# Storing the low parts of shared weights in DRAM for the second half, and two steps of the convolution and the SSD decay on ScalarE

## The chip, the cores and the metric

One core of a Trainium2 chip runs the kernel alone. The metric is the device time of one execution in microseconds. A core has five engines with queues of their own: TensorE (PE, with its weight loads PEld), VectorE (DVE), ScalarE (ACT), GpSimd (POOL) and SyncE (SP), which here issues nearly all transfers. Each engine takes its instructions in order and waits on semaphores for the others.

## The reference

One decoder layer over 1024 tokens of width 2048, all in float32. One input projection feeds three causal token mixers; their outputs are joined, projected back and normalised with the residual.

```python
h = einsum('bld,dn->bln', x, w_in)
y_s5  = s5_mixer(...) * silu(s5_z)
qk    = silu(causal_dwconv(ml_qk, ml_conv_w, ml_conv_b))       # 4 taps
y_ml  = mlstm_mixer(q, k, ml_v, ...) * silu(ml_z)
xbc   = silu(causal_dwconv(ssd_xbc, ssd_conv_w, ssd_conv_b))   # 4 taps
y_ssd = rms_norm(ssd_mixer(xs, bs, cs, ssd_dt, ...) * silu(ssd_z), ssd_norm_g)
out   = einsum('bln,nd->bld', concatenate([y_s5, y_ml, y_ssd]), w_out)
x     = layer_norm(ALPHA * x + out, ln_g, ln_b)

# in ssd_mixer, per chunk of 128 tokens and per head:
seg  = a_cum[:, :, :, None] - a_cum[:, :, None, :]
lmat = exp(where(causal, seg, -inf))
```

## The kernel before, in words

The matrix products keep float32 accuracy by splitting: each operand becomes a high part, rounded to the type fp32r that TensorE takes, and a low part, the rest. A product is three matmuls: high by high, high by low, low by high. The helper `split` (lines 170 to 172) makes the parts: ScalarE casts the raw tile to the high part, VectorE subtracts that from the raw tile.

The program has four stages. The first, to about 680 us of the profiled execution, computes part of the projections with sums and differences of blocks; it is not touched. Then `half(0)` and `half(1)` each treat 512 tokens: six column tiles qk, then fourteen tiles xbc, each a projection followed by the four-tap convolution and SiLU, while the mLSTM and SSD mixers run in between as background pieces. Last, `outproj(0)` and `outproj(1)` multiply 512 tokens each with the output weights, in four blocks of 512 columns (nb 0 to 3), and normalise.

Weights come in units of 512 KB (128 rows by 1024 floats), in the order of the list `W.plan`. `Weights.next` hands one out and emits the next: a transfer from DRAM into a raw tile `w<n>r` (three buffers, shared with the raw activation tiles x1r, y0r and y1r), then the split into `w<n>h` and `w<n>l` (three buffers each). Units w123 to w162 serve half 0 and w163 to w202 serve half 1 with the same 40 pieces of weights. Units w203 to w234 serve output projection 0; w235 to w274 serve output projection 1, with the same 32 pieces, of which the last eight come twice: in the last column block, token tiles 0 and 1 are done first (`op13a`, w259 to w266), then tiles 2 and 3 (`op13b`, w267 to w274). Three units, w270 to w272, have buffers of their own (`W.spare`).

In `conv` (line 353) ScalarE copies the projection out of PSUM into `stg`, VectorE multiplies by the first tap and adds the bias (line 359), then adds three more taps (line 361); ScalarE applies SiLU.

In `ssd_super`, for each of six heads of a group, a row of cumulated decays is spread over all partitions (tile `A`). `sel` takes its exponential into `E`. `mask` subtracts the column's own cumulated decay in four pieces of 128x128, bounded above by 0 (VectorE, line 469, with the negated sums `NC` from `cumulate`), takes the exponential (ScalarE, line 470) and multiplies by the masked products `cbs`.

The order on each engine is set by a scheduler that simulates the program; the code gives the order of emission. In names such as s00A the digits are the half and the SSD group.

Of the kernel before, what the change touches and what calls it, by code (L numbers as in the profile page):

```python
# [13 lines left out]
ALU = mybir.AluOpType  # L14
# [25 lines left out]
def hybrid_trunk(ctx: ExitStack, tc: tile.TileContext, a: dict, out: bass.AP, dbg=None):  # L40
# [186 lines left out]
    class Weights:  # L227
# [5 lines left out]
        def emit(self):  # L233
            if self.at in self.spare:
                (src, shape), n = self.plan[self.at], f"w{self.at}"
                self.at += 1
                r = raw(src, shape, n + "r")
                th, tl = ([gt(f"{n}{x}{i}", dtype=F32R) for i in range(2)] for x in "hl")
                for i in range(2):
                    split(r[:, i], th[i], tl[i])  # L240
                self.ready.append((th, tl))
                return


            (src, shape, *more), n = self.plan[self.at], f"w{self.at}"
            before, after, key = more or ((), (), 0)
            if src is not None:
# [34 lines left out]
    W = Weights()  # L282

    def plan_c(t):
        W.plan += [(a["w_c"][t, u], (P, 8, P)) for u in range(2)]

    def plan_t(src, N):
        W.plan += [(src[u], (P, 2, N)) for u in range(8)]

# [63 lines left out]
    def conv(ps, halo, cw, cb, t, dest, nm):  # L353
# [4 lines left out]
        c = gt(nm + "cv")  # L358
        dve.tensor_scalar(out=c, in0=stg[:, 0:HT], scalar1=cw[:, t, 0:1], scalar2=cb[:, t:t + 1], op0=ALU.mult, op1=ALU.add)
        for j in range(1, 4):  # L360
# [32 lines left out]
    def cumulate(h, LC):  # L393
# [4 lines left out]
        NC = sp.tile([P, 4, 36], F32, name=n + "NC", tag="NC")  # L398
        dve.tensor_scalar_mul(NC.rearrange("p c k -> p (c k)"), ps[:, :144], -1.0)
        pr = pm(n + "r")  # L400
        for c in range(4):
# [12 lines left out]
        act.copy(out=ir, in_=pt[64:68, :])  # L414
        return NC, b, lf, ir


    def ssd_super(h, sgp, tiles, gx, ys):

        n = f"s{h}{sgp}"  # L420
        DT, NC = gx
        xs, BT, CT = tiles[0:3], tiles[3:5], tiles[5:7]
# [39 lines left out]
        def mask(k):  # L462
# [3 lines left out]
            for c in range(4):  # L466
                sl = slice(c * P, (c + 1) * P)

                dve.tensor_scalar(out=Lm[:, sl], in0=Lm[:, sl], scalar1=NC[:, c, hd:hd + 1], scalar2=0.0, op0=ALU.add, op1=ALU.min)
            act.activation(out=Lm, in_=Lm, func=AF.Exp)  # L470
            if k % 3 == 0:
# [993 lines left out]
    for h in range(2):  # L1465
# [4 lines left out]
        for t in sg_tiles(1)[:3]:  # L1470
            plan_c(t)
        plan_t(a["w_x4"], HT)
    for nb in (0, 1, 2, 3, 0, 1, 2, 3, 3):
        plan_t(a["w_out"][nb], HT)

# [3 lines left out]
    def half(h, X, Xn):  # L1479
# [4 lines left out]
        def pre():  # L1484
# [3 lines left out]
            yield  # L1488
            NC, b, lf, ir = cumulate(h, LC)
            gx.extend([DT, NC])  # L1490
            yield
# [227 lines left out]
```

## Time and profile before

| | |
|---|---|
| Median of 3 runs | 1612.53 us (1611.51 to 1612.76) |
| Profiled execution | 1610.04 us, span 1608.3 us |
| TensorE clock granted | 0.994 |
| Busy: TensorE, VectorE, ScalarE, GpSimd | 1579.1, 1120.7, 658.2, 80.3 us |
| DRAM traffic | 271.74 MB read, 57.28 MB written |

The span goes from the first to the last instruction that the profiler shows. A row of the profile names the line, the engine, the operation, and the tiles as out<-in. A group of instructions has its count, busy time and mean duration in ns, and after the bar the idle time of its engine just before it with what ended it; `PE ms L571 <- DVE sm L566: 1.2, 1, 1.2` in a list of waits says that TensorE's instruction writing ms at line 571 waited for VectorE's writing of sm, 1.2 us in total, once, 1.2 at longest. In a timeline the first number is the start in us, the second the duration. A transfer's row gives its size and the time from issue to landing.

### The profile page before, as it was taken

Reading aid. Unit: us, or ns where it says so; the run is one execution under the profiler, and the core shown is the slowest. Engines: PE = TensorE matmul, PEld = TensorE weight load, DVE = VectorE, ACT = ScalarE, POOL = GpSimd, SP = SyncE. Lnnn points to the kernel's source line nnn. Section 1 sums busy time; section 2 is a strip of 40 time slices with the busy share of each in tenths; the row PEclk is TensorE's granted clock in tenths of the full one; section 3 lists DMA queues with packets and bytes.
Section 4 is the critical chain, followed back from the end, with each engine's and each line's share of the span. In section 5 each row is a group of like instructions: output and inputs, shape, how many; then the busy total and the mean of one; then the engine's idle time right before and its main releaser. Section 6 shows DMA issues by size and latency. Waiting matters only on the chain. (4 is left out here: it accounts for less than half of the span.)

```text
span 1608.3 us, 21146 instructions
## 1 busy us (share of the span) xinstructions
PE 1579.1 (98%) x7688; PEld 1329.4 (83%) x7688; DVE 1120.7 (70%) x1844; ACT 658.2 (41%) x927; POOL 80.3 (5%) x183
## 2 busy tenths in 40 slices
PE   9999999999999999999999999999999999999996
PEld 7898988987988888778888888788887888888884
DVE  5678978878868786565646788685697753484348
ACT  4333242147345556543542546364354331321222
POOL 0000000000001110001100000010000000000000
PEclk9999999999999999999999999999999999999998
DMA  8988777987987768364434553452654453575345
GB/s 318 328 320 316 255 269 251 306 293 223 336 302 248 247 227 275 130 223 127 137 105 159 183 169 119 151 171 66 217 195 145 132 194 118 183 242 160 129 144 183
DMA packets 139304, 333.56 MB, mean 207 GB/s; under 512 B 24489, under 2 KB 41001, under 8 KB 139201
## 3 DMA queue, kind: packets, MB, share of 16 engines
q1 hardware_dynamic: 129792, 317.54, 59.1%
q10 hardware_dynamic: 9408, 14.68, 2.6%
q8 instruction: 60, 0.98, 0.2%
q14 instruction: 44, 0.35, 0.1%
HBM read 271.74 MB, written 57.28 MB: 205 GB/s over the span
## 5 line engine op out<-in xcount | busy, mean ns | idle before, releaser
L1297 DVE TENSOR_TENSOR e<-e,b 128x512 f32<-128x512 f32 (+1 forms) x72 | 43.9, 645 | 3.7 <-PE b L1372 3.2
L1556 DVE SCALAR_TENSOR_TENSOR r<-r,mv,ln_g 128x512 f32<-128x512 f32 x32 | 23.1, 742 | 0.0
L1557 DVE SCALAR_TENSOR_TENSOR r<-r,lrs,ln_b 128x512 f32<-128x512 f32 x32 | 23.0, 742 | 0.0
L1576 DVE BATCH_NORM_STATS2 bst<-r 128x6 f32<-128x512 f32 x32 | 20.8, 682 | 0.0
L362 ACT ACT_TABLE_LOAD x15 | 19.2, 1283 | 3.7 <-DVE qc00cv L361 3.4
L1052 POOL COPY s5m0up<-s5m0u 128x256 f32<-128x256 f32 x2 | 0.8, 398 | 316.2 <-DMA s5m0u<-s5u 316.2
L1297 DVE TENSOR_TENSOR f<-f,b1c 128x512 f32<-128x512 f32 x15 | 9.4, 682 | 8.7 <-ACT f L1350 8.7
L172 DVE TENSOR_TENSOR y1l<-y1r,y1h 128x1024 fp32r<-128x1024 f32 x8 | 9.8, 1222 | 7.5 <-ACT y1h L171 7.5
L1277 ACT ACTIVATE f<-f 128x512 f32<-128x512 f32 x20 | 12.1, 628 | 6.2 <-DVE f L1297 3.2
L171 ACT CAST y1h<-y1r 128x1024 fp32r<-128x1024 f32 x8 | 8.4, 1053 | 9.1 <-PE op03p L344 9.1
L779 DVE TENSOR_TENSOR s5small<-s5small 128x32 f32<-128x32 f32 (+2 forms) x66 | 11.2, 195 | 0.7
L1548 ACT ACTIVATE lrs<-lrs 128x1 f32<-128x1 f32 x8 | 1.6, 202 | 24.4 <-DVE lrs L1547 24.4
L1297 DVE TENSOR_TENSOR f<-f,b2c 128x512 f32<-128x512 f32 x5 | 3.4, 687 | 11.6 <-PE b2c L1444 11.6
L172 DVE TENSOR_TENSOR y0l<-y0r,y0h 128x1024 fp32r<-128x1024 f32 x8 | 9.8, 1221 | 2.3 <-ACT y0h L171 2.2
L172 DVE TENSOR_TENSOR x1l<-x1r,x1h 128x1024 fp32r<-128x1024 f32 x8 | 9.8, 1219 | 2.3 <-ACT x1h L171 2.3
L731 DVE TENSOR_TENSOR sgo<-sgo,mzs 128x384 f32<-128x384 f32 x16 | 8.9, 555 | 2.3 <-DMA mzs<-zg 2.1
L171 ACT CAST y0h<-y0r 128x1024 fp32r<-128x1024 f32 x8 | 8.4, 1046 | 4.9 <-PE xbc_13p L1531 4.8
L1271 ACT ACT_TABLE_LOAD x8 | 10.3, 1283 | 0.1
L1270 ACT ACT_TABLE_LOAD x7 | 9.0, 1283 | 2.4 <-ACT e L1271 2.4
L1305 ACT COPY e<-b 128x512 f32<-128x512 f32 (+1 forms) x12 | 6.7, 558 | 7.5 <-PE b L1372 7.5
L1160 DVE TENSOR_TENSOR gsg<-gsg,gsz 128x512 f32<-128x512 f32 x8 | 5.5, 683 | 6.0 <-DMA gsz<-s5z 6.0
L741 PEld LDWEIGHTS mf<-ident,sgo 128*128 128x128 f32 x48 | 5.7, 140 | 4.7 <-DVE sgo L731 3.8
(4696 smaller groups left out, 5741.1 us busy)
## 6 DMA issues: line engine op xcount, KB each, us to landing
xn<-in_x_dram SPq DMA_DIRECT2D x32, 256.0 KB, 5.5
out_dram<-r SPq DMA_DIRECT2D x32, 256.0 KB, 3.8
x1r<-in_xT_dram SPq DMA_DIRECT2D x8, 512.0 KB, 4.3
y0r<-mixT SPq DMA_DIRECT2D x8, 512.0 KB, 3.3
y1r<-mixT SPq DMA_DIRECT2D x8, 512.0 KB, 3.5
vd<-e SPq DMA_DIRECT2D x16, 192.0 KB, 4.0
szd<-f ACTq DMA_DIRECT2D x12, 256.0 KB, 3.0
vx<-vd SPq DMA_DIRECT2D x8, 384.0 KB, 4.3
```

The costliest lines, as they stand in the source:

```text
L171: act.copy(out=th, in_=raw)
L172: dve.tensor_sub(out=tl, in0=raw, in1=th.bitcast(F32))
L362: act.activation(out=dest, in_=c, func=AF.Silu)
L731: dve.tensor_mul(out=sg, in0=sg, in1=sz)
L779: eng.tensor_tensor(out=o, in0=i, in1=j, op=op)
L1270: act.activation(out=c[:, 0:256], in_=c[:, 0:256], func=AF.Silu)
L1271: act.activation(out=c[:, 256:512], in_=c[:, 256:512], func=AF.Sigmoid)
L1277: act.activation(out=c, in_=c, func=AF.Silu)
L1297: dve.tensor_tensor(out=o, in0=x, in1=y, op=op)
L1556: dve.scalar_tensor_tensor(out=o, in0=o, scalar=mv[:, 0:1], in1=lng[nb], op0=ALU.subtract, op1=ALU.mult)
L1557: dve.scalar_tensor_tensor(out=o, in0=o, scalar=rs, in1=lnb[nb], op0=ALU.mult, op1=ALU.add)
L1576: dve.bn_stats(out=st[t][:, nb, :], in_=r[t][nb])
```

## The change

Of the 80 units whose weights an earlier unit already had (w163 to w202, w235 to w274), the low part is no longer computed. The first unit with these weights stores its low part in DRAM (72 units, 512 KB each); a later one loads it into `w<n>l` while the raw tile is loaded and cast as before. The first convolution tap with its bias becomes an ACTIVATE with the function Identity on ScalarE. The decay bound becomes a Relu on ScalarE, with the sign turned: Relu(sum - A) and then Exp with scale -1; `cumulate` also keeps the sums unnegated, as PC.

```diff
--- before.py
+++ after.py
@@ -232,17 +232,29 @@
 
         def emit(self):
             if self.at in self.spare:
-                (src, shape), n = self.plan[self.at], f"w{self.at}"
+                (src, shape, _, low_), n = self.plan[self.at], f"w{self.at}"
                 self.at += 1
                 r = raw(src, shape, n + "r")
                 th, tl = ([gt(f"{n}{x}{i}", dtype=F32R) for i in range(2)] for x in "hl")
                 for i in range(2):
-                    split(r[:, i], th[i], tl[i])
+                    act.copy(out=th[i], in_=r[:, i])
+                    sync.dma_start(out=tl[i].bitcast(F32), in_=low_[:, i])
                 self.ready.append((th, tl))
                 return
 
 
             (src, shape, *more), n = self.plan[self.at], f"w{self.at}"
+            if more and more[0] in ("keep", "kept"):
+                r = raw(src, shape, n + "r")
+                th, tl = self.parts()
+                if more[0] == "keep":
+                    split(r, th, tl)
+                    sync.dma_start(out=more[1], in_=tl.bitcast(F32))
+                else:
+                    act.copy(out=th, in_=r)
+                    sync.dma_start(out=tl.bitcast(F32), in_=more[1])
+                self.ready.append((th, tl))
+                return
             before, after, key = more or ((), (), 0)
             if src is not None:
                 self.chains[key] = Chain(src, shape, n)
@@ -281,11 +293,23 @@
 
     W = Weights()
 
+
+    lows = {}
+
+    def plan_low(key, src, shape):
+        if key in lows:
+            W.plan.append((src, shape, "kept", lows[key]))
+        else:
+            lows[key] = dr.tile(list(shape), F32, name=f"low{key}", tag=f"low{key}")
+            W.plan.append((src, shape, "keep", lows[key]))
+
     def plan_c(t):
-        W.plan += [(a["w_c"][t, u], (P, 8, P)) for u in range(2)]
-
-    def plan_t(src, N):
-        W.plan += [(src[u], (P, 2, N)) for u in range(8)]
+        for u in range(2):
+            plan_low(f"c{t}_{u}", a["w_c"][t, u], (P, 8, P))
+
+    def plan_t(nm, src, N):
+        for u in range(8):
+            plan_low(f"{nm}{u}", src[u], (P, 2, N))
 
     def proj_c(X, nm):
 
@@ -356,7 +380,7 @@
         pool.tensor_copy(out=stg[:, 0:3], in_=halo[:, t, :])
         pool.tensor_copy(out=halo[:, t, :], in_=stg[:, HT:HT + 3])
         c = gt(nm + "cv")
-        dve.tensor_scalar(out=c, in0=stg[:, 0:HT], scalar1=cw[:, t, 0:1], scalar2=cb[:, t:t + 1], op0=ALU.mult, op1=ALU.add)
+        act.activation(out=c, in_=stg[:, 0:HT], func=AF.Identity, scale=cw[:, t, 0:1], bias=cb[:, t:t + 1])
         for j in range(1, 4):
             dve.scalar_tensor_tensor(out=c, in0=stg[:, j:j + HT], scalar=cw[:, t, j:j + 1], in1=c, op0=ALU.mult, op1=ALU.add)
         act.activation(out=dest, in_=c, func=AF.Silu)
@@ -397,6 +421,8 @@
         pe.matmul(ps[:, :144], lhsT=tri, rhs=LC[:, :, 0:36], start=True, stop=True)
         NC = sp.tile([P, 4, 36], F32, name=n + "NC", tag="NC")
         dve.tensor_scalar_mul(NC.rearrange("p c k -> p (c k)"), ps[:, :144], -1.0)
+        PC = sp.tile([P, 4, 36], F32, name=n + "PC", tag="PC")
+        act.copy(out=PC.rearrange("p c k -> p (c k)"), in_=ps[:, :144])
         pr = pm(n + "r")
         for c in range(4):
             pe.matmul(pr[0:36, c * P:(c + 1) * P], lhsT=LC[:, c, 0:36], rhs=tri, start=True, stop=True)
@@ -412,13 +438,13 @@
         act.copy(out=lf, in_=pt[32:36, :])
         ir = gt(n + "ir", (4, HT))
         act.copy(out=ir, in_=pt[64:68, :])
-        return NC, b, lf, ir
+        return NC, PC, b, lf, ir
 
 
     def ssd_super(h, sgp, tiles, gx, ys):
 
         n = f"s{h}{sgp}"
-        DT, NC = gx
+        DT, PC = gx
         xs, BT, CT = tiles[0:3], tiles[3:5], tiles[5:7]
         dtx = hp.tile([P, 4, 6, 64], F32, name=n + "dx", tag="dx")
         Bt, cbs = [None] * 2, [None] * 2
@@ -466,8 +492,8 @@
             for c in range(4):
                 sl = slice(c * P, (c + 1) * P)
 
-                dve.tensor_scalar(out=Lm[:, sl], in0=Lm[:, sl], scalar1=NC[:, c, hd:hd + 1], scalar2=0.0, op0=ALU.add, op1=ALU.min)
-            act.activation(out=Lm, in_=Lm, func=AF.Exp)
+                act.activation(out=Lm[:, sl], in_=Lm[:, sl], func=AF.Relu, scale=-1.0, bias=PC[:, c, hd:hd + 1])
+            act.activation(out=Lm, in_=Lm, func=AF.Exp, scale=-1.0)
             if k % 3 == 0:
                 wdx[gg] = hp.tile([P, 4, 3, 64], F32, name=n + f"wd{gg}", tag="wd", bufs=2)
             nw = 3 if h == 1 else 4
@@ -1469,9 +1495,9 @@
             plan_c(t)
         for t in sg_tiles(1)[:3]:
             plan_c(t)
-        plan_t(a["w_x4"], HT)
+        plan_t("x", a["w_x4"], HT)
     for nb in (0, 1, 2, 3, 0, 1, 2, 3, 3):
-        plan_t(a["w_out"][nb], HT)
+        plan_t(f"o{nb}_", a["w_out"][nb], HT)
 
     W.spare = {len(W.plan) - 8 + i for i in (3, 4, 5)}
 
@@ -1486,8 +1512,8 @@
             DT, LC = gates(h, G)
             yield
             yield
-            NC, b, lf, ir = cumulate(h, LC)
-            gx.extend([DT, NC])
+            NC, PC, b, lf, ir = cumulate(h, LC)
+            gx.extend([DT, PC])
             yield
             yield from ml_gates(h, G, NC, b, lf, ir, mlg)
         bg.add(pre(), 1.5)
```

On ScalarE, in the first SSD group of half 0, around the cast of w158. Before:

```order
L171 CAST x1h_7988<-x1r_7986 128x1024
L171 CAST w158h<-w158r 128x1024
L457 ACT_TABLE_LOAD
L457 ACTIVATE s00E_7947<-s00A_7935 128x512
L443 COPY s00cbs_7997<-s00cb_7992 128x512
L458 COPY s00El<-s00E_7947 128x4
L450 COPY s00Bt_8005<-s00bt_8000 128x512
```

And now:

```order
L495 ACTIVATE s00A_8057<-s00A_8057,cu0PC 128x128 x3
L469 COPY s00cbs_8184<-s00cb_8179 128x512
L496 ACTIVATE s00A_8057<-s00A_8057 128x512
L476 COPY s00Bt_8192<-s00bt_8187 128x512
L495 ACTIVATE s00A_8118<-s00A_8118,cu0PC 128x128 x4
L483 ACTIVATE s00E_8202<-s00A_8132 128x512
L496 ACTIVATE s00A_8118<-s00A_8118 128x512
L484 COPY s00El<-s00E_8202 128x4
L171 CAST w158h<-w158r 128x1024
L171 CAST x1h_8240<-x1r_8238 128x1024
```

The cast of w158 stood ahead of the first exponential of the group; now it stands behind the bounds of the first three heads (12 pieces, of which the rows show the last seven), their exponentials and the fourth s00E.

On SP, in the last column block of output projection 1. Before, raw loads follow each other:

```order
L1570 DMA xn_13173<-in_x_dram 128x512
L1570 DMA xn_13175<-in_x_dram 128x512
L209 DMA w264r<-in_w_out_dram 128x1024
L209 DMA w265r<-in_w_out_dram 128x1024
L209 DMA w266r<-in_w_out_dram 128x1024
L209 DMA w267r<-in_w_out_dram 128x1024
L209 DMA w268r<-in_w_out_dram 128x1024
L209 DMA w269r<-in_w_out_dram 128x1024
L209 DMA w270r<-in_w_out_dram 128x1024
L209 DMA w271r<-in_w_out_dram 128x1024
```

And now each unit has a load of its low part beside the raw one:

```order
L1596 DMA xn_13321<-in_x_dram 128x512
L1596 DMA xn_13323<-in_x_dram 128x512
L255 DMA w262l<-lowo_3_214 128x1024
L209 DMA w264r<-in_w_out_dram 128x1024
L255 DMA w263l<-lowo_4_215 128x1024
L209 DMA w265r<-in_w_out_dram 128x1024
L255 DMA w264l<-lowo_5_216 128x1024
L255 DMA w265l<-lowo_6_217 128x1024
L209 DMA w266r<-in_w_out_dram 128x1024
L255 DMA w266l<-lowo_7_218 128x1024
L209 DMA w267r<-in_w_out_dram 128x1024
L255 DMA w267l<-lowo_0_211 128x1024
```

A low load waits for the buffer that the unit three before held, so for TensorE; the raw loads behind it on the queue wait with it.

On SP a little later, where the results of tiles 0 and 1 are stored too (out_dram). Before:

```order
L209 DMA w272r<-in_w_out_dram 128x1024
L1558 DMA out_dram<-r_12573 128x512
L1558 DMA out_dram<-r_12861 128x512
L209 DMA w273r<-in_w_out_dram 128x1024
L1558 DMA out_dram<-r_13143 128x512
L209 DMA w274r<-in_w_out_dram 128x1024
L1558 DMA out_dram<-r_13317 128x512
```

And now:

```order
L1584 DMA out_dram<-r_12721 128x512
L1584 DMA out_dram<-r_13009 128x512
L209 DMA w270r<-in_w_out_dram 128x1024
L1584 DMA out_dram<-r_13291 128x512
L209 DMA w271r<-in_w_out_dram 128x1024
L241 DMA w270l_13523<-lowo_3_214 128x512
L241 DMA w270l_13524<-lowo_3_214 128x512
L1584 DMA out_dram<-r_13465 128x512
L241 DMA w271l_13542<-lowo_4_215 128x512
L241 DMA w271l_13543<-lowo_4_215 128x512
L209 DMA w272r<-in_w_out_dram 128x1024
L209 DMA w273r<-in_w_out_dram 128x1024
```

The load of w270r stands behind two stores and the low part of w269; before, it was two places ahead of the last xn loads.

On TensorE, in the same place, w267 and w268 are used up for both tiles 2 and 3 before w269 begins; before, tile 2 ran ahead of tile 3. The last matmul of tile 2 is now seven matmuls ahead of the end, where it was sixteen.

## The prediction, on record before the changed kernel ran

> **What bounds the kernel now.** I read the page's busy times first, then what TensorE waits for from 880 us on, where the second half and the output projection run, then the tail in order of time.
>
> ```profile
> span 1608.3 us, 21146 instructions
> PE 1579.1 (98%) x7688; PEld 1329.4 (83%) x7688; DVE 1120.7 (70%) x1844; ACT 658.2 (41%) x927; POOL 80.3 (5%) x183
> ```
>
> TensorE is busy nearly throughout, VectorE is not. So what VectorE loses is worth only the waits that TensorE has on it:
>
> ```profile
> PE ms L571 <- DVE sm L566: 1.2, 1, 1.2
> PE op00p L343 <- ACT xb113st L355: 1.1, 1, 1.1
> PE s01xt L433 <- DVE s01dx L434: 0.9, 1, 0.9
> PE op13bp L321 <- ACT w274h L171: 0.4, 1, 0.4
> PE mf L741 <- DVE sgo L731: 0.3, 1, 0.3
> ```
>
> That is all of it, 3.9 us from 880 us to the end, of which 2.4 us name VectorE. TensorE eats a weight unit (512 KB raw) at two paces:
>
> ```profile
> L343 PE MATMUL op10p<-w235h,y1h x8: 389/389/389, 1418.2 to 1423.0; 128*128 128x512 f32 x8
> L343 PE MATMUL op10p<-w236h,y1h x8: 389/389/389, 1423.7 to 1428.4; 128*128 128x512 f32 x8
> L343 PE MATMUL op13ap<-w259h,y1h x4: 389/389/389, 1548.8 to 1550.8; 128*128 128x512 f32 x4
> L343 PE MATMUL op13ap<-w260h,y1h x4: 389/389/389, 1551.5 to 1553.5; 128*128 128x512 f32 x4
> ```
>
> One unit lasts 5.5 us (1418.2 to 1423.7) until the last column block; there, from 1548.8, each unit serves two row tiles instead of four and lasts 2.7 us. What the memory side can do, and what waiting in line costs:
>
> ```profile
> 40.00:80.00 40.00, 40.00 (x184) 34.10 (x183) 24.87 (x45) 15.68 (x20) 0.96 (x3) 1.00 0.91 326
> 1420.59 0.33 SPq L209 DMA_DIRECT2D w238r<-in_w_out_dram  x1
> 1420.97 1.85 SPq L1570 DMA_DIRECT2D xn<-in_x_dram  x4
> 1422.92 0.38 SPq L209 DMA_DIRECT2D w239r<-in_w_out_dram  x1
> w238r<-in_w_out_dram SPq DMA_DIRECT2D x1, 512.0 KB, 3.5
> w239r<-in_w_out_dram SPq DMA_DIRECT2D x1, 512.0 KB, 6.9
> ```
>
> The first row (time, busy times, clock, DMA share, GB/s) is the densest stretch of the kernel: 326 GB/s at a share of 0.91, so about 358 GB/s if full (326/0.91, an estimate). A 512 KB load lands in 3.5 us; behind four loads of 256 KB (1.05 MB) it took 6.9, so 1.05 MB cost 3.4 us, or 308 GB/s.
>
> **The change part by part.** Rows for its prices:
>
> ```profile
> 1413.28 1.23 DVE L172 TENSOR_TENSOR w235l<-w235r,w235h 128x1024 fp32r<-128x1024 f32 x1 [3.50 <-ACT w235h L171]
> L359 DVE TENSOR_SCALAR xb05cv<-xb05st,cols x1: 547/547/547, 901.0 to 901.0; 128x512 f32<-128x512 f32 x1
> L362 ACT ACTIVATE xc<-xb05cv x1: 631/631/631, 905.7 to 905.7; 128x512 f32<-128x512 f32 x1
> L469 DVE TENSOR_SCALAR s00A<-s00A,cu0NC 128x128 f32<-128x128 f32 x24 | 6.3, 310 | 0.7 <-ACT s00E L457 0.7
> L681 ACT ACTIVATE m1jk<-m1hm 128x192 f32<-128x192 f32 x16 | 5.8, 368 | 0.3
> L458 ACT COPY s00El<-s00E 128x4 f32<-128x4 f32 x6 | 1.2, 196 | 0.1
> ```
>
> Removed from VectorE: the subtractions of 80 units (98 us at 1.23), 40 first taps (22 us at 0.547), 96 decay bounds (30 us at 0.31). It lay beside TensorE's 98%. Of the waits, ms and s01xt stood behind such work; I credit 1.5 of their 2.1 us, between nothing and 2.1. The mf wait stays with the transfers that feed sgo. Taken: -1.5.
>
> Added to ScalarE: 40 taps at about 0.63 (25 us) and 96 bounds of 128x128. No row has that shape; 128x4 at 0.196 and 128x192 at 0.368 bound it, and I take 0.3, nearer the larger (29 us), plus two copies PC of that size. ScalarE has room in sum (41%), but runs in order, and in the first SSD group of half 0 the cast of w158 now stands behind three decay bounds:
>
> ```profile
> 908.62 1.05 ACT L171 CAST w158h<-w158r 128x1024 fp32r<-128x1024 f32 x1 [1.18 <-DMA w158r<-in_w_x_dram]
> 909.69 1.28 ACT L457 ACT_TABLE_LOAD   x1
> 910.98 0.63 ACT L457 ACTIVATE s00E<-s00A 128x512 f32<-128x512 f32 x1
> 919.08 0.62 ACT L457 ACTIVATE s00E<-s00A 128x512 f32<-128x512 f32 x1
> L1529 PE MATMUL xbc_8p<-p13h,w158h x2: 389/389/389, 919.8 to 922.5; 128*128 128x512 f32 x2
> ```
>
> The fourth s00E starts at 919.08 now; in the new order the cast follows it, an Exp and a small copy, so at about 919.1 + 0.6 + 0.6 + 0.2 = 920.5, done at 921.5. Adding it up from the first s00E at 910.98 gives nearly the same: 12 bounds, six more Exps, copies and a cast are some 10.5 us. TensorE wants w158 at 919.8. Late by 1.7 us; if the first s00E starts earlier because the cast no longer precedes it, nothing; with bounds of 0.368 and a slower row transfer, 4. Taken: +2. The same order in half 1 has its low parts from DMA, not from a subtraction behind the cast; I take nothing there. The wait op00p <- ACT xb113st stays: three taps more ahead of that copy, but its conv inputs come earlier; +-1, taken as 0.
>
> The Trainium skill speaks against this move: "ScalarE: Activation LUTs", Rules for kernel authors, puts relu, add and min on VectorE and budgets 0.3 us an ACTIVATE plus 0.83 ns an element. By that (estimate) a bound would cost 0.41 us, w158 would be 1.3 us later and the sum 1.3 higher; the trace's 128x512 at 0.63 is below its 0.72.
>
> Stores, 72 of 512 KB: each waits on SP for a subtraction, and the next raw load stands behind it. Where a load also had to wait for that subtraction to free its buffer, nothing new waits; it lands later by the store, 0.52 MB, 1.5 to 1.7 us at 358 to 308 GB/s. How far ahead a unit is ready, at a roomy and at the tight place:
>
> ```profile
> L171 ACT CAST w259h<-w259r x1: 1055/1055/1055, 1538.1 to 1538.1; 128x1024 fp32r<-128x1024 f32 x1
> 1419.34 1.23 DVE L172 TENSOR_TENSOR w236l<-w236r,w236h 128x1024 fp32r<-128x1024 f32 x1 [0.72 <-ACT w236h L171]
> ```
>
> w259 is cast by 1539.2 and used at 1548.8, 9.6 us later; w236, beside the y1 loads, is ready at 1420.6 and used at 1423.7, 3.1 later. One store ahead of a load (1.7) fits under both; two in a row (3.4) would cost 0.3 at the tight place, and a chain of five keeping units there 3 at most. Between 0 and 3, nearest the single store: +0.5.
>
> Loads of kept low parts, 80: each waits on SP until TensorE has finished the unit three before, and what is queued behind waits too. At 5.5 us a unit there are 11 us from issue to need for a 3.5 us transfer: covered. If that cover is gone (two transfers ahead, 6.9 us) it still holds. In the last block it does not hold:
>
> ```profile
> 1567.65 0.33 SPq L209 DMA_DIRECT2D w270r<-in_w_out_dram  x1
> 1550.00:1560.00 10.00, 10.00 (x46) 8.28 (x45) 5.67 (x6) 3.34 (x5) 0.00 (x0) 1.00 0.54 170
> 1570.32 0.39 PE L345 MATMUL op13ap<-w266h,y1l 128*128 128x512 f32 x1
> ...
> 1589.41 0.39 PE L323 MATMUL op13bp<-w274h,y1l 128*128 128x512 f32 x1
> ...
> 1593.05 0.39 PE L323 MATMUL op13bp<-w274h,y1l 128*128 128x512 f32 x1
> ...
> 1590.09 0.68 DVE L1575 SCALAR_TENSOR_TENSOR r<-xn,op13bp 128x512 f32<-128x512 f32 x1
> 1603.72 1.41 DVE L1557 SCALAR_TENSOR_TENSOR r<-r,lrs,ln_b 128x512 f32<-128x512 f32 x2
> ```
>
> From 1550 to 1560 the kernel moves 170 GB/s. With low parts a unit is 1.05 MB per 2.7 us: 385 GB/s of weights alone, above 358. From 1548.8, when w259 starts, w258 is done and w261's low load may go, there follow 14 low and 11 raw loads, four xn and five output stores by SP's order: 25 x 0.524 + 9 x 0.262 = 15.5 MB. At 358 GB/s that is 43.3 us, plus 2 us fixed (3.5 less 1.5): w274's low part lands at 1594.1. Twelve matmuls of 0.23 us follow: TensorE ends at 1597, now 1593.4. At 308 GB/s it is 1604. Besides, w270r, now issued at 1567.65, moves behind w269's low load (slot free when w266 ends, 1570.7) and two stores that wait for VectorE's normalisation.
>
> VectorE's tail: from tile 2's evacuation it has 20 operations some 0.66 us apart (two overlap into 1.41) and 0.9 us of small ones, 14.0 us; the work of tiles 0 and 1 is done by then. Now it runs from 1590.1 to 1605.1 with two operations of theirs among it. Tile 2 ends 1.6 us before TensorE in the new order (3.6 now). So the last VectorE operation ends at 1597 - 1.6 + 0.3 + 14.0 = 1609.7 instead of 1605.1: +4.6. With 308 GB/s it is +11.6. With transfers hidden TensorE ends near 1593 and it is +0.5: the eight subtractions gone here buy nothing, because tile 2 comes later. Taken: +5, near the denser rate.
>
> Sum: -1.5 + 2 + 0.5 + 5 = +6. The profiled execution took 1610.04 (span 1608.3), the median of the runs is 1612.53, 2.5 higher; +6 gives a span of 1614 and a median of 1618.5.
>
> **Rivals.** Transfers hidden in the tail: single slices of the trace pass 358 GB/s, though no long stretch does. With the tail at +0.5 the sum is +1.5, or 1614. "DMA: Bandwidth & Descriptors" of the Trainium skill, under Bandwidth, measures 425 GB/s for 16 MB with the pair's other core idle, and gives about 358 per core from HBM; by the first this rival holds, by the second the forecast; the 326 at 0.91 agrees with the second.
>
> Faster: ScalarE's cast of w158 comes in time and VectorE's relief ends all its waits, 2.4 us, op00p's 1.1 too since its conv tiles finish earlier, and w274's. That is 1608.6. It decides at the tail: low loads must land within the 5.4 us from slot to need, and against it stand 385 GB/s.
>
> More transfers late: after 1425 us 16 output stores and 8 xn loads (6.3 MB) join 1.05 MB per 5.5 us; over 45 us 14.9 MB, 331 GB/s, as dense as the densest stretch. If low loads are late there and in the keeping passes, 5 more with the tail at 308: 1625 to 1629.
>
> **How the numbers follow.** A measurement here cannot tell less than 0.2% (3.2 us) from no change: slower begins at 1615.8, faster ends at 1609.3. Chances: forecast 0.54 (own range 1614 to 1623, 0.06 of it within 0.2%), hidden transfers 0.19, faster 0.12, more late 0.15. So slower 0.63, same 0.25, faster 0.12. Range 1610 to 1626: from just above the faster case to the foot of the worst.
>
> **What would show it.** DVE near 970 us busy, ACT near 710. In the tail: DMA share above 0.85 from 1550 to 1590, TensorE waits on low loads of w269 to w274, its end after 1596. A wait of TensorE on w158h or w158l near 920. No wait on ms. If the tail's transfers take under 5 us with TensorE ending by 1594, the forecast is wrong by its largest term; if TensorE waits spread over 1240 to 1540, the cover of 11 us was.

## The result and the profile after

The changed kernel takes 1631.88 us (median of 4 runs, 1628.86 to 1637.84) against 1612.64 us before: a ratio of 1.0130, 95% interval 1.0108 to 1.0152. The profiled execution took 1633.76 us, its span is 1632.0. The prediction had slower, but 1618.5 with a range to 1626: the sign was right, the size less than a third of what came. The page's span and busy times:

```profile
span 1632.0 us, 21292 instructions
PE 1588.0 (97%) x7688; PEld 1336.1 (82%) x7688; DVE 996.4 (61%) x1625; ACT 715.5 (44%) x1063; POOL 65.5 (4%) x183
```

VectorE lost 124 us of work (1120.7 before; forecast were 970 and, for ScalarE, 710), and that bought nothing. TensorE's waits from 880 us to the end (total, times, longest) were 3.9 us before. Now:

```profile
PE mf L767 <- DVE sgo L757: 3.6, 4, 1.7
PE s01xt L459 <- DVE s01dx L460: 3.1, 1, 3.1
PE ms L597 <- DVE sm L592: 2.6, 1, 2.6
PE op13bp L345 <- ACT w270h L240: 2.3, 1, 2.3
PE op13bp L346 <- DMA w270l<-lowo: 1.8, 1, 1.8
PE s01sp L516 <- DVE s01wd L500: 1.6, 1, 1.6
PE s01y L540 <- DVE s01S L523: 1.4, 2, 0.9
PE op00p L367 <- ACT xb113st L379: 1.1, 1, 1.1
```

Five of the eight name VectorE, whose load went down; at the places that are followed below it is late because its operands are. Two of the eight lie in the tail, five in the second half's mixer, one at the head of the output projection. After some of these waits TensorE also runs slower for a while (stretch, busy times of PE, PEld, DVE, ACT and POOL, clock, DMA share, GB/s; the 3.1 us wait s01xt ends at 967.2, the 2.6 us wait ms at 1050.9):

```profile
960.00:965.00 5.00, 4.09 (x23) 3.25 (x21) 3.30 (x4) 3.98 (x6) 0.42 (x2) 1.00 0.62 211
965.00:970.00 5.00, 2.78 (x8) 2.35 (x9) 3.94 (x7) 3.34 (x6) 0.42 (x2) 0.63 0.95 366
970.00:975.00 5.00, 5.00 (x23) 4.34 (x22) 2.91 (x4) 0.95 (x2) 0.19 (x1) 0.69 0.25 98
1050.00:1055.00 5.00, 4.13 (x10) 2.87 (x11) 3.43 (x5) 2.60 (x3) 0.00 (x0) 0.66 0.05 16
1596.00:1606.00 10.00, 5.91 (x19) 4.15 (x18) 4.55 (x7) 2.88 (x6) 0.00 (x0) 0.83 0.98 362
```

Where the time went is read best from the starts of TensorE's first matmul on a weight unit. The table gives before's time and, for this kernel and the experiments below, how much later the unit is reached in the profiled execution. Units w123 to w162 are the first half's projections, w163 to w202 the second half's, w203 on the output projection, w259 on the last column block. Ahead of w123 only e13 and e10 change anything, so what the others show there is the spread between executions: differences between columns count, and they too only from some 5 us on. e15, whose time is that of the kernel before, goes from +3.2 to +7.9 in the execution that was profiled.

| | w123 | w163 | w176 | w203 | w214 | w259 | TensorE's end | ratio to before (95%) |
|---|---|---|---|---|---|---|---|---|
| before (us) | 697.3 | 955.3 | 1043.4 | 1228.4 | 1302.8 | 1548.8 | 1593.4 | 1 |
| after | +1.2 | +1.9 | +12.1 | +17.0 | +16.5 | +17.3 | +23.1 | 1.0130 (1.0108 to 1.0152) |
| e1 ScalarE moves | +2.3 | +0.7 | +3.8 | +5.1 | +5.9 | +5.9 | +6.1 | 1.0036 (1.0020 to 1.0053) |
| e2 low parts | +1.1 | +2.6 | +7.5 | +10.4 | +13.7 | +13.7 | +19.2 | 1.0123 (1.0097 to 1.0150) |
| e3 bound | +1.9 | +2.7 | +2.0 | +3.2 | +3.4 | +3.4 | +3.8 | 0.9999 (0.9986 to 1.0011) |
| e4 tap | +1.5 | +1.7 | -0.3 | +0.6 | -0.6 | -0.6 | -0.3 | 0.9987 (0.9973 to 1.0001) |
| e5 loads from ScalarE | +1.0 | +4.2 | +7.3 | +14.8 | +20.8 | +22.9 | +34.0 | 1.0179 (1.0146 to 1.0212) |
| e6 half alone | +1.6 | +4.8 | +7.4 | +12.0 | +17.1 | +17.4 | +17.2 | 1.0089 (1.0065 to 1.0114) |
| e7 output alone | +4.4 | +3.9 | +4.2 | +4.1 | +2.6 | +3.5 | +9.4 | 1.0036 (1.0024 to 1.0048) |
| e8 stores alone | +2.9 | +5.0 | +9.2 | +10.5 | +8.8 | +8.8 | +8.7 | 1.0036 (1.0023 to 1.0048) |
| e11 8 KB stores | +1.2 | +0.8 | -0.0 | +1.4 | +1.0 | +2.5 | +2.7 | 1.0002 (0.9990 to 1.0014) |
| e17 256 KB stores | +6.0 | +6.7 | +11.3 | +11.3 | +10.7 | +10.7 | +11.3 | 1.0040 (1.0022 to 1.0058) |
| e18 stores one unit later | +1.3 | +6.1 | +11.4 | +12.1 | +14.0 | +19.0 | +19.4 | 1.0110 (1.0088 to 1.0132) |
| e14 half's loads alone | +2.6 | +2.5 | +1.6 | +5.1 | +10.4 | +10.4 | +10.8 | 1.0070 (1.0055 to 1.0086) |
| e12 output, no tail | -0.9 | -1.1 | -0.8 | -1.0 | -2.3 | -1.8 | -0.8 | 1.0009 (0.9995 to 1.0024) |
| e15 output, no tail, and tap | +3.2 | +3.7 | +2.4 | +5.3 | +4.0 | +4.7 | +7.9 | 0.9999 (0.9987 to 1.0010) |
| e13 wide buffer | +8.3 | +10.5 | +11.6 | +15.0 | +14.8 | +18.6 | +19.3 | 1.0082 (1.0067 to 1.0097) |
| e10 wide buffer, waits | +9.7 | +10.8 | +11.7 | +14.7 | +15.3 | +19.1 | +19.6 | 1.0101 (1.0085 to 1.0116) |

The changed kernel loses 15 us between w163 and w203 (1.9 to 17.0), nothing from there to w259, and 5.8 us in the tail (17.3 to 23.1). The tail was forecast, the 15 us were not.

Waits of TensorE make up most of the 15: between w163 and w203 the five in the mixer come to 12.3 us, where before's three there (ms, s01xt, mf) came to 2.4. The lower clock is the rest: over the five-us stretches behind s01xt (0.63 and 0.69), ms (0.66) and mf (0.93 and 0.73, from 1160 on) it costs some 7 us, an estimate from these figures; before, no such stretch from 955 to 1229 is below 1.00. The two together come to a little more than the 15.

### The profile page after: what moved, and what is told of

Its sections match the earlier page's. It is cut to its first block, busy times and chain, and to the rows that moved or that the text cites. A ratio compares the mean times of both kernels' runs of the same rounds, so it can differ in the third digit from the quotient of the medians.

```text
span 1632.0 us, 21292 instructions
## 1 busy us (share of the span) xinstructions
PE 1588.0 (97%) x7688; PEld 1336.1 (82%) x7688; DVE 996.4 (61%) x1625; ACT 715.5 (44%) x1063; POOL 65.5 (4%) x183
## 4 chain that ended last, share of the span: by engine, by line
PE 80%; DMA 10%; DVE 6%; ACT 2%; issue 1%; SPq 1%; DVEq 0%; POOL 0%; ACTq 0%
PE b L1397 8%; PE b L1398 8%; PE b L1396 8%; DMA sgo<-og 1%; PE op01p L367 1%; PE op10p L367 1%; PE op01p L368 1%; PE op10p L368 1%; PE op12p L369 1%; PE op12p L367 1%; PE op11p L367 1%; PE op02p L369 1%; PE op02p L368 1%; PE op11p L369 1%; PE op01p L369 1%
## 5 line engine op out<-in xcount | busy, mean ns | idle before, releaser
L1582 DVE SCALAR_TENSOR_TENSOR r<-r,mv,ln_g 128x512 f32<-128x512 f32 x32 | 22.9, 740 | 0.0
L701 DVE SCALAR_TENSOR_TENSOR st_m<-st_m,m1dec,m1o 96x193 f32<-96x193 f32 x12 | 4.9, 410 | 17.9 <-PE m1o L697 17.9
L171 ACT CAST y1h<-y1r 128x1024 fp32r<-128x1024 f32 x8 | 8.4, 1054 | 15.6 <-PE op03p L368 14.8
L1303 ACT ACTIVATE f<-f 128x512 f32<-128x512 f32 x20 | 12.1, 628 | 6.2 <-DVE f L1323 3.3
L767 PE MATMUL mf<-ident,sgo 128*128 128x128 f32 x48 | 9.1, 287 | 3.9 <-DVE sgo L757 3.8
L755 DVE SCALAR_TENSOR_TENSOR sgo<-m1hm,m1nd,sgo 128x192 f32<-128x192 f32 x16 | 5.9, 412 | 11.1 <-DMA sgo<-og 11.1
L504 DVE TENSOR_TENSOR s01E<-s01E,xc 128x512 f32<-128x512 f32 x6 | 5.0, 831 | 11.6 <-ACT s01El L484 11.6
```

The lines of the kernel that those rows point to most:

```text
L1582: dve.scalar_tensor_tensor(out=o, in0=o, scalar=mv[:, 0:1], in1=lng[nb], op0=ALU.subtract, op1=ALU.mult)
```

## The experiments

**Which part: ScalarE's moves or the low parts.** The whole change taken apart: e1 has only the two moves to ScalarE, e2 only the low parts, e3 and e4 one move each. The edits are those of the change itself, the lines not named stay as before:

```diff
 e1, e3:  -dve.tensor_scalar(... NC ..., op0=ALU.add, op1=ALU.min)   +act.activation(... func=AF.Relu, scale=-1.0, bias=PC ...)
 e1, e4:  -dve.tensor_scalar(out=c, ...)                             +act.activation(out=c, ... func=AF.Identity ...)
 e2:      the hunks of emit, plan_low, plan_c, plan_t
```

> Only the two moves to ScalarE (decay bound and first tap), every low part computed as before. The whole change took 19 us more. Theory A, the queue of ScalarE: the 15 us that TensorE loses between 955 and 1245 us come from the longer chain through ScalarE, so this kernel takes 10 to 15 us more than before (1622 to 1628) and shows the waits s01xt, s01sp, ms. Theory B, the low loads: the row and norm transfers wait on SP behind low loads that wait for TensorE; then this kernel is within 3 us of before (1610 to 1616).

> Only the low parts through DRAM; bound and first tap on VectorE as before. Theory A: the tail's 6 us and at most 3 more, 1617 to 1622, and no wait s01xt or ms beyond before's. Theory B: 17 to 23 us more than before, 1630 to 1636, with the mixer's first 300 us as late as in the whole change.

> Only the decay bound on ScalarE (96 operations that the whole change shows at 0.39 us, 1.57 a head against VectorE's 1.24). Theory A: 5 to 9 us more than before, 1617 to 1622, with waits on s00wd, s01wd and s01S (the state and output products of a head) and little on s01xt. Theory B: no change, 1611 to 1614.

> Only the first convolution tap on ScalarE (0.80 us there against 0.55 on VectorE). Theory A: 4 to 8 us more than before, 1616 to 1621, by the wait s01xt and the idle VectorE between taps. Theory B: no change, 1611 to 1614.

Measured: e1 1619.52, e2 1633.63, e3 1613.16, e4 1610.21 us, before 1613.37 beside them. Theory A falls: the low parts alone make the whole change's loss, and each ScalarE move alone costs nothing that can be measured. e1 itself lies between what the two theories gave (1622 to 1628 and 1610 to 1616): both moves together cost 0.36%. In e1's waits of TensorE stand the casts behind the bounds in ScalarE's line, as the prediction had it, but at w168 and w169 in the second half; the cast of w158 stays ahead of the first group there (907.79):

```profile
PE op00p L343 <- ACT xb113st L355: 2.4, 1, 2.4
PE qk_2p L300 <- DVE w168l L172: 1.3, 1, 1.3
PE qk_3p L298 <- ACT w169h L171: 0.7, 1, 0.7
```

**Which low parts, and stores or loads.** e6 keeps the low parts of the projections alone, e7 those of the output projection alone, e8 the stores alone.

```diff
 e6:  -plan_low(f"{nm}{u}", src[u], (P, 2, N))     (for w_out; w_x4 stays)   +W.plan.append((src[u], (P, 2, N)))
 e7:  the same for w_c and w_x4, w_out stays
 e8:  -act.copy(out=th, in_=r); sync.dma_start(out=tl..., in_=more[1])       +split(r, th, tl)
 e5:  -sync.dma_start(out=tl.bitcast(F32), in_=more[1])                      +act.dma_start(out=tl.bitcast(F32), in_=more[1])
```

> e2 with each low load issued by ScalarE right behind the cast of the same unit instead of by SP (only w270 to w272, which use other buffers, stay on SP). The bytes are the same; the wait for TensorE to free the buffer now stands behind a cast that waits for the same unit. Theory B1, SP's line: what costs are small transfers (s01A, szs, sgo) that stand on SP behind a low load that waits for TensorE. Then 9 to 14 us of e2's 20 go and only the tail and the stores stay: 1618 to 1624. Theory B2, bytes: the small transfers are late because half as much again is moved on the same 16 engines. Then nothing moves: 1630 to 1636.

> e2 with the 40 low parts of the projections alone; the output projection computes its low parts as before. By the places where TensorE waits in e2, s01xt 2.3 us, ms 5, mf 3.5, op00p 4.5 lie in the second half and 4.3 in the tail, so under B1 and B2 alike 10 to 15 us more than before, 1623 to 1628. If the tail is the greater part, 1613 to 1618.

> e2 with the low parts of the output projection alone (32 stored, 40 loaded). The tail's late low loads stay, 4 to 6 us, and part of the wait op00p, which stands where the first stores begin: 1617 to 1623, by both theories. If the whole change's loss were made by the half's transfers and handed on to the end, 1611 to 1615.

> Only the stores: 72 low parts are written to DRAM, and the second half computes its own as before. The prediction's term for the stores was 0.5 us, between 0 and 3: 1611 to 1616. If the stores, which wait on SP for VectorE's subtraction, hold back the row and mixer transfers as the low loads do, 5 to 10 us: 1618 to 1623.

Measured: e6 1629.03, e7 1619.81, e8 1620.27, e5 1642.76 us, before 1613.64. The parts add up: e6 and e7 are 0.89% and 0.36%, e2 is 1.23%. e8's loss lies where the first half's stores end: +2.9 at w123, +9.2 at w176, and none of the 32 later stores adds to it (+10.5 at w203, +8.8 at the end). e5 took SP's waits for TensorE away and came out slower yet, above both of its expectations. In its tail, 11.1 us later instead of 5.5, the low loads now stand behind casts that wait for raw loads; in the half it loses more than e2 too. So those waits on SP are not what costs, or the same wait costs no less on ScalarE.

How a store costs is seen at the end of the first half. SP's line in e8 (SPq, the issue of transfers), then ScalarE there, then the same two places before:

```profile
948.09 0.33 SPq L251 DMA_DIRECT2D lowx<-w162l  x1
948.51 0.38 SPq L209 DMA_DIRECT2D w163r<-in_w_c_dram  x1
...
954.93 1.05 ACT L171 CAST w163h<-w163r 128x1024 fp32r<-128x1024 f32 x1 [7.18 <-DMA w163r<-in_w_c_dram]
956.84 0.58 ACT L377 COPY xb08st<-xbc_8p 128x512 f32<-128x512 f32 x1
960.82 1.05 ACT L171 CAST w164h<-w164r 128x1024 fp32r<-128x1024 f32 x1 [2.92 <-DMA w164r<-in_w_c_dram]
963.19 0.63 ACT L384 ACTIVATE xc<-xb08cv 128x512 f32<-128x512 f32 x1
```

Before:

```profile
941.23 0.33 SPq L209 DMA_DIRECT2D w163r<-in_w_c_dram  x1
944.66 1.05 ACT L171 CAST w163h<-w163r 128x1024 fp32r<-128x1024 f32 x1 [3.77 <-DMA w163r<-in_w_c_dram]
951.49 0.58 ACT L355 COPY xb08st<-xbc_8p 128x512 f32<-128x512 f32 x1
955.83 0.63 ACT L362 ACTIVATE xc<-xb08cv 128x512 f32<-128x512 f32 x1
```

The stretches around it (busy times, clock, share, GB/s), first in e8, then before:

```profile
945.00:950.00 5.00, 5.00 (x25) 4.26 (x24) 3.10 (x7) 2.00 (x2) 0.00 (x0) 1.00 0.90 312
```

```profile
940.00:945.00 5.00, 5.00 (x25) 4.25 (x24) 4.42 (x12) 1.23 (x2) 0.00 (x0) 1.00 0.46 138
```

TensorE is already 5.0 us behind at w163 in this execution, so 5.0 comes off each difference. Counted so, w163r leaves 2.3 us later (948.51 against 941.23) and takes 6.4 us to its cast where it took 3.4; the cast is 5.3 us later (954.93 against 944.66), and ScalarE, which runs in order, sits idle 7.18 us on it. The copy xb08st behind it is hardly later, 0.3 us. The loss grows on the next unit: w164r leaves only when VectorE has subtracted w163l (957.27 against 947.00), and its cast, with another 2.92 us idle, now stands ahead of the SiLU of xb08, which comes 2.4 us later (963.19 against 955.83). From that SiLU hangs s01dx, 3.3 us later, for which TensorE then waits 3.7 us (0.9 before), though w163 itself is ready 3.6 us ahead. The unit that is delayed is in time; the unrelated work behind it in line is not.

**Waits or bytes.** e10 keeps the waits of the half's loads and moves 4 KB, e11 keeps those of the stores and moves 8 KB. e9 was meant to keep the bytes without the wait, e12 leaves the tail's low loads out.

```diff
 e9, e16:  +sync.dma_start(out=d, in_=src)      d a DRAM tile; from w163 on (e9), up to w162 (e16)
 e10:      -wp.tile(shape, ..., tag="wl")       +wide = wp.tile([P, 8 * P + 8], ..., tag="wl")
           +sync.dma_start(out=wide[:, 8 * P:].bitcast(F32), in_=tiny[0])     from w163 on
 e13:      e10 without its dma_start
 e11:      -sync.dma_start(out=more[1], in_=tl...)   +sync.dma_start(out=more[1][0:16, 0, 0:128], in_=tl[0:16, 0, 0:128]...)
 e12:      e7 +W.plan[-8:] = [p[:2] for p in W.plan[-8:]]
```

> The kernel before, with 40 copies of 512 KB from the weights to DRAM added on SP, one behind the raw load of each unit from w163 to w202, that wait for no engine and that nobody reads: the bytes and the places in SP's line of the half's low loads, without their wait for TensorE. Theory B2, bytes and places in the line: the mixer's small transfers (szs, sgo, rows) come late as in e6, 6 to 11 us more than before (1619 to 1625), waits ms and mf. Theory B1, the wait for TensorE: 1612 to 1615.

> The kernel before, with a 4 KB load on SP in the place of each of the half's 40 low loads, into 8 columns added to the low part's buffer, so that it waits for TensorE to free that buffer as the low load does; the low part is subtracted on VectorE as before, behind this small load (at most about 1 us later). Theory B1: 6 to 11 us more than before, 1619 to 1625. Theory B2: 1612 to 1616.

> e8 with 16 rows of 128 elements stored (8 KB) in the place of 512 KB: the 72 waits of SP for VectorE's subtraction stay, the bytes go. If the waits make the 6.6 us of e8, this is 1617 to 1622 with s01xt waiting 3 us or more; if the bytes make them, 1612 to 1615.

> e7 with the last eight units (w267 to w274) computing their own low parts as before; 32 low parts of the output projection are still stored and 32 loaded. If the 6 us of e7 are the tail's low loads that come later than TensorE wants them, 1612 to 1616 without waits on w269 to w274. If they lie in the stores and in the loads before the tail, 1617 to 1621.

Measured: e9 1615.41, e10 1630.29, e11 1613.69, e12 1613.50 us, before 1613.99. e12 settles the tail: without the last eight low loads the output projection's low parts cost nothing that can be measured, so e7's 0.36% is the tail. e11 settles that SP's wait for VectorE's subtraction costs nothing that can be measured. e9 says nothing on the question: its copies depend on no work, so they were placed between 110 and 481 us, far ahead of their units. e10 lies above both of its expectations, and half of its loss is there at w123 already (+9.7), where it loads nothing yet, so it needed a control.

**The control, and loads without stores.** e14 lets the half load each low part from one of two stored ones; e16 is e9's idea for the stores; e15 joins what e12 and e4 left.

```diff
 e14:  e6, stores only of w123 and w155 (one.append(more[1]));   -in_=more[1]   +in_=one[...]
 e15:  e12 and the first tap on ScalarE
```

> e10 without its 4 KB loads: the low part's buffers of the projections are 8 columns wider than before, nothing else is changed. If e10's 16 us come from the buffers' place (its 128x512 matmuls take 0.003 us more from start to start, 5740 of them), 1626 to 1631, and SP's waits for TensorE cost under 3. If they come from the waits, 1612 to 1615.

> e6 with two stores in the place of 40: the second half loads each of its 40 low parts from one stored part of the same shape, so bytes and waits of the loads stay and those of the stores go (the loaded values are those of two units). If loads and stores add up, e6's 15.4 less e8's 6.6: 8 to 10 us more than before, 1621 to 1625, with waits op00p and mf and without s01xt's. If the loads cost only beside the stores, 1612 to 1617.

> The kernel before with 40 copies of 512 KB from the weights to DRAM on SP in the first half, behind the raw load of each unit from w123 to w162, waiting for no engine. If the bytes of the stores make e8's 6 us before w176, 1617 to 1621, with s01xt waiting 3 us; if it takes bytes behind a wait, 1612 to 1615 as e9 for the second half.

> e12 (low parts of the output projection through DRAM but for the last eight units) with the first convolution tap on ScalarE, which e4 showed at 0.9987 of before. If VectorE's relief is worth its waits, 1608 to 1611; if it lies beside TensorE's work, 1611 to 1615.

Measured: e13 1626.30, e14 1623.82, e16 1615.48, e15 1613.25 us (1.0070 for e14, 0.9999 for e15, interval 0.9987 to 1.0010), before 1613.07. e13 takes nearly all of e10's time, so SP's waits for TensorE alone cost 0.19% by the medians, which is not told from nothing: the intervals of the two overlap. e16 failed as e9 did, its copies going out from 110 to 479 us; all that e9 and e16 show is that as many copies where nothing hangs on them cost little (both 1.0011). e14's 0.70% and e8's 0.36% give 1.06%, e6 has 0.89% (0.65 to 1.14): stores and loads add. e15 says what VectorE's relief is worth where nothing is lost: nothing that can be measured, though it relieves VectorE only in part (32 subtractions and 40 taps, 1066.6 us busy against 1120.7).

e14's loss comes late in the half, at +5.1 by w203 and +10.4 by w214. TensorE's greatest wait and what ScalarE does ahead of it:

```profile
PE op00p L371 <- ACT xb113st L383: 3.3, 1, 3.3
```

```profile
1230.54 1.05 ACT L171 CAST w204h<-w204r 128x1024 fp32r<-128x1024 f32 x1 [5.13 <-DMA w204r<-in_w_out_dram]
1231.49 0.58 ACT L383 COPY xb18st<-xbc_8p 128x512 f32<-128x512 f32 x1
```

It is the same pattern as at w163: ScalarE waits 5.13 us in the cast of w204, a unit that reads no stored low part here, and the convolution's copies stand behind. Before the change it waited 2.78 us there; TensorE is 5.1 us later at w203, and counted from there w204r leaves 3.2 us later (1225.93 against 1217.65). Behind the wait the clock was 0.60 and 0.71 for ten microseconds (1240 to 1250), so the loss is larger than the wait. In the changed kernel this wait is 1.1 us as before: the parts add up by their times, not by the same waits.

The wait mf is VectorE waiting for sgo and mzs, sixteen loads of 192 KB. In e14 it is 2.0 us, no more than in kernels that load no low part in the half (0.2 to 2.2 in e3, e4, e8, e11, e13, e15, e17 and e18); the 2.7 of e2, 3.0 of e6 and 3.6 of the changed kernel lie above that. In e2 a low load leaves ahead of them at 1144.10, when TensorE has done with w188, and SP then also waits for earlier transfers to land, which it doesn't before the change in that stretch. SP's line and one of its waits in e2, then the first and last of the eight issues before:

```profile
1144.10 0.33 SPq L255 DMA_DIRECT2D w191l<-lowc  x1
...
1146.41 0.47 SPq L750 DMA_DIRECT2D sgo<-og  x1
...
1153.46 0.32 SPq L751 DMA_DIRECT2D mzs<-zg  x1
```

```profile
SPq L751 <- DMA ln_b<-in_ln_b_dram: 1.6, 2, 1.4
```

```profile
1138.93 0.43 SPq L726 DMA_DIRECT2D sgo<-og  x1
1143.16 0.43 SPq L727 DMA_DIRECT2D mzs<-zg  x1
```

The eight issues take 4.2 us before (1138.93 to 1143.16), 7.1 in e2 and 6.3 in e14. That this makes the longer mf is argued, not shown.

**Bytes or place.** The last two runs vary the stores alone.

```diff
 e17:  e8, -sync.dma_start(out=more[1], in_=tl...)    +sync.dma_start(out=more[1][0:64], in_=tl[0:64]...)
 e18:  e8, +held.append((more[1], tl)); if len(held) > 1: the store of held.pop(0)
```

> e8 with 64 of 128 rows stored, 256 KB in the place of 512: each store keeps its place and its wait for VectorE. If the bytes on the shared 16 engines cost, in proportion, half of e8's 6.6: 1615 to 1618. If the cost begins only where a delay is no longer covered (the cast of w163, which TensorE's s01xt hangs on), 1612 to 1615.

> e8 with each store issued one unit later: at the tight place the stores of w158 and w160 to w162 then stand behind the raw loads of w159 and w161 to w163 and not ahead of them, the bytes are the same. If raw loads and rows late behind stores are the cause, 1612 to 1616 and s01xt waits under 2 us. If the bytes are, 1618 to 1622 as e8.

Measured: e17 1618.61, e18 1630.58 us, before 1612.31. Both expectations of e17 miss: half the bytes cost as much as all (1.0040 and 1.0036; half of 0.36% lies just below e17's interval), and 8 KB cost nothing that can be measured. Both of e18 miss too: with the same bytes and the raw loads ahead of the stores, the loss is three times e8's. There ScalarE waits for three raw loads in a row, and s01xt waits 4.1 us; a third of the loss comes at the head of output projection 1, where w235r leaves at 1428.09 (1418.48 in e8) and TensorE waits for VectorE's r, which it doesn't in e8:

```profile
ACT w162h L171 <- DMA w162r<-in_w_x_dram: 5.9, 1, 5.9
ACT w163h L171 <- DMA w163r<-in_w_c_dram: 5.2, 1, 5.2
ACT w164h L171 <- DMA w164r<-in_w_c_dram: 3.9, 1, 3.9
PE op10p L368 <- DVE r L1600: 3.2, 2, 2.3
```

The three raw loads do not explain the threefold loss: the same waits are 4.2, 7.2 and 2.9 in e8, and up to w203 e8, e17 and e18 are level (+10.5, +11.3, +12.1). So the place in SP's line matters, and from 256 KB on more than the bytes do; which place is good can't be told from the order alone. What makes 256 KB cost as much as 512 was not tried. Copies of 512 KB that stay at the loads' places and wait for nothing weren't achieved either, so bytes without any wait remain untested there.

## Why the prediction was wrong, step by step

**The step that failed: "Loads of kept low parts, 80 ... covered", and beside it "Stores ... +0.5".** Both compare a unit's transfer with TensorE's need for that unit: 11 us from issue to need against 3.5, 3.1 us ahead against 1.7. For the low loads that held: no wait of TensorE from w163 to w259 names one in the changed kernel. For the stores the text did look at the raw load behind, but again only at the need for its own unit, and with 1.7 us of delay; w163r's cast came 5.3 us later in e8, and the unit was still in time. What failed is what stands behind. The text itself said that "what is queued behind waits too", and priced it at nothing. Behind stand raw loads, token loads, sgo and mzs; ScalarE and VectorE, which take them, work in order, and TensorE's second half hangs on those by short chains: s01xt waits 3.7 us in e8, op00p 3.3 in e14. Measured: stores 0.36% (some 6 us, forecast 0.5, bound 3), the half's low loads 0.70% (11 us, forecast 0). The cover to look for was that of every transfer behind the new one in line, not that of the new one.

**VectorE's relief, -1.5, and "No wait on ms".** Right where the relief stands alone: in e1, e4 and e15, which move the first tap to ScalarE and add no transfers in the half, TensorE waits at neither ms nor s01xt. In time that is worth nothing that can be measured (e4 0.9987, interval to 1.0001). Wrong in the changed kernel: ms went from 1.2 to 2.6 us, s01xt from 0.9 to 3.1. These waits name VectorE, but it waited for operands. s01xt is 2.1 to 4.1 us in every kernel that stores 256 KB or more of each unit in the first half, and 0.8 with the loads alone (e14). For ms, in e2, the szs loads stand behind a low load of the same stretch (w176l at 1033.28, szs from 1034.59), and VectorE gets to the gating 6.6 us after they leave instead of 4.7 (e2, then before):

```profile
1033.28 0.32 SPq L255 DMA_DIRECT2D w176l<-lowc  x1
1034.59 1.04 SPq L586 DMA_DIRECT2D szs<-szd  x2
...
1041.15 0.69 DVE L587 TENSOR_TENSOR s01yt<-s01yt,szs 128x512 f32<-128x512 f32 x1 [6.59 <-DMA szs<-szd]
```

```profile
1032.91 0.87 SPq L562 DMA_DIRECT2D szs<-szd  x2
1037.65 0.69 DVE L563 TENSOR_TENSOR s01yt<-s01yt,szs 128x512 f32<-128x512 f32 x1 [5.19 <-DMA szs<-szd]
```

VectorE sat idle 5.19 us for szs before the change too: the row that would have warned. The low load ahead is not the whole cause, though: e14 has one there as well, VectorE gets to the gating 5.7 us after, and ms waits 1.2 us as before. What else adds in e2 is open.

**ScalarE, +2 at w158.** Right in place and nearly in size. In the changed kernel the cast of w158 runs from 920.94 to 921.98 (forecast 920.5 to 921.5), and TensorE, 0.6 us behind at w157, is 2.3 behind at w158: 1.7 late, as forecast. The list of waits shows 0.9 of it, as s00sp, whose four matmuls now stand ahead of w158's. What failed is "The same order in half 1 ... I take nothing there": it looked at the low parts, which come from DMA, and not at what else hangs on the bounds. There VectorE waits for ScalarE's s01A behind them, and TensorE 1.6 us at s01sp and 1.4 at s01y, two waits that e2 and e14 do not show:

```profile
920.94 1.04 ACT L171 CAST w158h<-w158r 128x1024 fp32r<-128x1024 f32 x1
995.88 0.43 DVE L500 TENSOR_TENSOR s01wd<-s01dx,s01A 128x256 f32<-128x256 f32 x1 [2.85 <-ACT s01A L496]
```

The durations of a bound and a tap, both longer than was taken:

```profile
L495 ACT ACTIVATE s00A<-s00A,cu0PC x24: 384/390/400, 912.6 to 931.5; 128x128 f32<-128x128 f32 x24
L383 ACT ACTIVATE xb08cv<-xb08st,cols x1: 818/818/818, 953.3 to 953.3; 128x512 f32<-128x512 f32 x1
```

A bound takes 0.390 us against 0.3 taken, above the upper row of 0.368, and a tap 0.818 against 0.63: the SiLU of the same shape, which gave the price, has no scale and bias from columns. Instructions of ScalarE overlap, however: four bounds in a row are one entry of 1.28 us in the trace, 0.30 from start to start, so what was taken for the line of bounds was right. By the Trainium skill ("ScalarE: Activation LUTs", Rules for kernel authors) the estimate for a bound had been 0.41, and another section of that page, What ACT_TABLE_LOAD costs, adds 93 ns for each operand taken from a column to 186 ns and 0.833 ns an element: 0.39 for the bound and 0.80 for the tap (estimates). The trace agrees with the latter in both. In time these moves add nothing to the low parts that can be told (1.0130 against e2's 1.0123, the intervals overlap); whether part of the 0.36% that they cost alone comes on top can't be told either.

**The tail, +5.** Right: TensorE's end moves 5.8 us between w259 and the end, e7's 0.36% less e12's 0.09% is some 4 us, the last waits name w270 as forecast, and the tail's transfers run at 362 GB/s with a share of 0.98, beside the 358 that the sum used. What was not foreseen is that TensorE isn't held before 1596 (10.00, 10.00 and 9.99 us busy of each ten from 1566 on): the low loads keep pace until four of the output's stores and w270's raw load, issued at 1592.64, join them.

**op00p stays, 0.** Right for the whole change (1.1 us, as before), by luck: in e2 and e14 it is 3.1 and 3.3.

**The rivals.** "More transfers late" had the right kind of cause and nearly the time (1625 to 1629). It named "the keeping passes" too, and e8's loss does lie at the end of one; but its sum stood on the output projection after 1425 us, by a mean rate of 331 GB/s over 45 us. The cover held there (+17.0 at w203, +17.3 at w259). A mean rate was the wrong test: the stretch behind the delay of w163r is five us long, the one at 0.90 above.

## What to carry to other kernels

A new transfer on a shared in-order queue is priced by what stands behind it, and by what stands behind the engine that takes that: follow the queue ten places on and ask for each entry how long before its need it lands now. Waits that name an engine are no credit for relieving it, until its own idle time just before shows that it was busy and not waiting for data. Taking 124 us of work from an engine that bounds nothing gave nothing here, and the kernel with the transfers that replaced it takes 1.3% longer.

## What the runs showed of the hardware

A buffer 8 columns (32 bytes a partition) wider made the whole kernel 0.82% slower (e13). In its profiled execution TensorE is 8.3 us behind at w123, 15.0 at w203 and 19.3 at the end. Its 128x512 matmuls vary where they were all alike (min/median/max ns, the same unit before and in e13), and from 1450 to 1540 us they start 230.3 ns apart on average instead of 226.7, which over 5740 of them is some 20 us (an estimate):

```profile
L343 PE MATMUL op11p<-w250h,y1h x8: 389/389/389, 1499.8 to 1504.6; 128*128 128x512 f32 x8
```

```profile
L353 PE MATMUL op11p<-w250h,y1h x8: 387/394/397, 1517.7 to 1522.5; 128*128 128x512 f32 x8
```

The widening also moves every buffer behind it; which of the two it is was not tried.

A wait of some 3 us often costs more than itself. After s01xt's 3.1 us the granted clock was 0.63 and 0.69 for the ten microseconds shown above, after ms's 2.6 us it was 0.66 for five; in e2, after ms had waited 3.1 us, it was 0.50 for five:

```profile
1045.00:1050.00 5.00, 4.81 (x9) 3.15 (x10) 2.69 (x5) 1.24 (x2) 0.00 (x0) 0.50 0.02 6
```

It need not: in e2 TensorE waited 1.0 and 3.1 us for op00p within six us, and the clock stayed at 1.00.

```profile
1245.00:1250.00 5.00, 2.48 (x14) 2.13 (x15) 4.82 (x8) 1.93 (x4) 0.62 (x2) 1.00 0.74 252
```

The waits of about 1 us before the change left it at 1.00. The Trainium skill ("TensorE: Matmul & The Clock Gate", Part 1: The HAM clock gate) has the clock halved after an idle window of some 3.4 us in a free-running count; these rows agree in kind, at somewhat shorter waits and not every time. Over the span the mean granted clock fell from 0.994 to 0.991, some 5 us of the 24 by which the span grew (0.009 x 1632.0 less 0.006 x 1608.3). Between w163 and w203, where it had been 1.00 throughout, the slower stretches cost some 7.
